# Root of the attention norm on the output projection's rows, in banks of its own; its weight in w_out

## The chip, the cores and the metric

The kernel runs on one core of a Trainium2 chip. Five engines work side by side, each with its own queue in fixed order: PE (matrix products and transposes, which write to PSUM), DVE and ACT (elementwise work, from SBUF and PSUM), POOL (elementwise work from SBUF, and DMA issues) and SP (DMA issues). They wait for one another by semaphores. The metric is the device time of one execution in microseconds; the time of a kernel is the median of three runs.

## The reference, cut to what matters

One decoder layer over 1024 tokens of width 1024, in float32. The token mixer has two halves of width 512, windowed attention with sinks and a gated recurrence (HGRN2). Each is normalised, then both go through one output projection:

```python
attn = sliding_window_sink_attention(aq, ak, av, attn_sinks[l])
attn = rmsnorm(attn, attn_out_w[l])          # y * rsqrt(mean(y*y) + eps) * w, over 512 columns
...
rec = rmsnorm(rec, hg_norm_w[l]) * jax.nn.silu(hg.reshape(B, T, HG_HEADS, HG_HEAD_DIM))
mix = jnp.concatenate([attn, rec], axis=-1) @ w_out[l]
x = x + g1 * rmsnorm(mix, post_w_mix[l])
h = rmsnorm(x, pre_w_mlp[l]) * (1.0 + sc2) + sh2
u = jnp.square(jax.nn.relu(h @ w_up[l]))
x = x + g2 * rmsnorm(u @ w_down[l], post_w_mlp[l])
```

The root of the attention norm is one number for each token; its weight is one number for each of the 512 columns, which are rows 0 to 511 of `w_out`.

## The kernel before, in words

Every float32 operand of a large product is kept as a high and a low part, and a product is three PE products: high by high, high by low, low by high (`proj3`). A helper records every operation, so that all rows of the profile have one line (L39); they are told apart by tiles.

The 1024 tokens are eight row blocks (tb) of 128. The stages on PE follow one another and overlap at their seams: input projection and attention (to about 200 us), the recurrence's units (to about 390), the output projection (about 365 to 465), then the up and the down projection of the channel mixer, which are arranged in seven products of blocks, to 1085.

**Attention** is a generator with four pieces for each row block; value projections (`pv`) are put between the pieces of different blocks to fill PE. The output of a block, `oT`, is transposed: columns on the partitions, tokens along the free dimension. Its norm takes these steps: ACT squares `oT` (`sqa`); DVE multiplies `oT` by the norm weight into `a3` (profile: `q<-oT,c_attw`); DVE sums the squares over four column blocks (`sqr`); PE transposes that (`ssp`); DVE sums to one number for each token (`ssc`); POOL makes the root (`t_att`, `r_att`); DVE puts it on a diagonal (`dg`); PE multiplies a matrix of ones by this diagonal, which spreads the root over all partitions (`rb`); DVE multiplies `a3` by it (`q<-q,rb`).

**Output projection.** `load_wo` splits `w_out` into parts, DVE and POOL making the low parts in turn. `op_prep` splits the attention (part 0) and the recurrence (part 1) of a row block; `op_mm` puts both parts of one half of the 1024 output columns into one bank (`po`): part 0 starts the sum, part 1 goes on with it. `out_proj` then has ACT square the bank, POOL make the root, DVE multiply the bank by root and weight (into `mixn`), add `x`, and so on to the normalised row block for the channel mixer.

**Transposes for the channel mixer.** `second_raw(0)` transposes row blocks 0 to 3, `second_raw(1)` blocks 4 to 7: eight tiles (`x2T`) of four transposes each, which ACT reads (`bt..h`) and then DVE or ACT reads (`h`).

**PSUM** has eight banks of 128 × 512 float32. The pool of `mm_ps` has two, that of `tp_ps` five, that of `a_ps` one. Scores, `pT`, `oT`, `po` and most `x2T` tiles take theirs from `tp_ps` in turn; `ssp`, `rb` and every third `x2T` tile (2 and 5) take the one of `a_ps`. A tile waits until the last reader of the bank's former tile is done.

**The order on each engine** is written out by hand up to the start of attention. From there on (`pin(False, ...)`) a scheduler sets it when the program is built, by its own idea of the times; what is moved in the source can therefore move other instructions as well. On the chip each engine takes its instructions in that order.

Of the kernel before, what the change touches and what calls it, by code (L numbers as in the profile page):

```python
# [47 lines left out]
def hybrid_layer(ctx: ExitStack, tc: tile.TileContext, I, out, dbg=None):  # L48
    nc = tc.nc
    ACT, DVE, POOL, PE, SP = (Queue(tc, e) for e in (nc.scalar, nc.vector, nc.gpsimd, nc.tensor, nc.sync))  # L50
# [9 lines left out]
    tiny1 = ctx.enter_context(tc.tile_pool(name="tiny1", bufs=1, side="right"))  # L60
# [25 lines left out]
    def t_(name, shape=(P, 512), dt=F32):  # L86
        return T2.tile(list(shape), dt, tag="t2", name=name)
# [4 lines left out]
    def tp_ps(name):  # L92
        return pb.tile([P, 512], F32, tag="b", name=name)
# [21 lines left out]
    ident, cT, bT, prew1, prew2 = (tab[:, a:b] for a, b in ((0, P), (P, 136), (136, 184), (184, 192), (192, 200)))  # L115
    ones = const.tile([P, P], F32, tag="ones", name="ones")
# [5 lines left out]
    mhalf = tiny0.tile([P, 8], F32, tag="mhalf", name="mhalf")  # L122
# [119 lines left out]
    def load_raw(mk, name, src, eng=None):  # L242
        rw = mk(name)
        (eng or SP).dma_start(rw, src)
        return rw

    def load_split(mk, name, src, eng=None, raw=None):
        hi, lo = mk(name + "h", dt=F32R), mk(name + "l", dt=F32R)
        for c in range(0, src.shape[1], 512):
            rw = load_raw(raw_, f"{name}r{c}", src[:, c:c + 512]) if raw is None else raw  # L250
            hc = hi[:, c:c + 512]
            ACT.activation(hc, rw, AF.Copy)
            (eng or DVE).tensor_tensor(lo[:, c:c + 512], rw, hc.bitcast(F32), ALU.subtract)
        return hi, lo

    gw1 = const.tile([P, D], F32, tag="gw1", name="gw1")
# [260 lines left out]
    attw = cload("attw", [P, 4], pool=tiny1)  # L517
    mle = cload("mle", [P, P], I32, pool=XA)
    fle = cload("fle", [P, P], pool=XA)
    attT = [None] * TB  # L520
    kTs, vs = {}, {}

    def attention(tb):
# [11 lines left out]
        aw = q  # L535
        a3 = aw.rearrange("p (m t) -> p m t", m=4)
# [5 lines left out]
        for mp in range(2):  # L542
            scs = [tp_ps(f"sc{tb}_{mp}_{g}").rearrange("p (m j) -> p m j", m=2) for g in range(2)]
            for m in range(2):
                for src in (tb - 1, tb) if tb else (tb,):
                    for g in range(2):
# [3 lines left out]
                                  start=True, stop=True)  # L550
# [48 lines left out]
        DVE.tensor_tensor(a3, o_ps.rearrange("p (m t) -> p m t", m=4), attw.unsqueeze(2).broadcast_to([P, 4, P]), ALU.mult)  # L599
        sqr = small.tile([P, P], F32, tag="sqr", bufs=1, name=f"sqr{tb}")  # L600
        DVE.tensor_reduce(sqr, sq.rearrange("p (m t) -> p t m", m=4), AX.X, ALU.add)
        ssp = pa.tile([P, 512], F32, tag="aps", name=f"ssp{tb}")
        PE.transpose(ssp[:, 0:P], sqr, ident)
        ssc = small.tile([P, 1], F32, tag="ssc", name=f"ssc{tb}")
        DVE.tensor_reduce(ssc, ssp[:, 0:P], AX.X, ALU.add)
        r = rstd_of(ssc, 512, 1, f"att{tb}")
        dg = small.tile([P, P], F32, tag="dg", bufs=1, name=f"dg{tb}")
        DVE.tensor_scalar(dg, ident, r[:, 0:1], None, ALU.mult)
        yield
        rb = pa.tile([P, 512], F32, tag="aps", name=f"rb{tb}")  # L610
        PE.matmul(rb[:, :P], lhsT=ones, rhs=dg, start=True, stop=True)
        DVE.tensor_tensor(a3, a3, rb[:, :P].unsqueeze(1).broadcast_to([P, 4, P]), ALU.mult)
        attT[tb] = aw
        yield

    def step(tb):
# [3 lines left out]
    att = [attention(tb) for tb in range(TB)]  # L620
# [15 lines left out]
    for tb in range(4):  # L636
        eng = DVE if tb < 2 else POOL
# [71 lines left out]
    aps = pa.tile([P, 512], F32, tag="aps", name="aps")  # L709
# [155 lines left out]
    wo = [[], []]  # L865
    op_mx, op_ps = {}, {}

    wo_raw = {}

    def wo_block(half, k):  # L870
        return I["w_o"][k][:, half * 512:half * 512 + 512]

    def load_wo(half, ks=range(KB)):
        for k in ks:
            wo[half].append(load_split(hT_, f"wo{k}_{half}", wo_block(half, k), eng=POOL if k % 2 else DVE,
                                       raw=wo_raw.pop((half, k), None)))

    def op_prep(tb, part):
        if (tb, part) in op_mx:
# [18 lines left out]
    def op_mm(tb, half, part, mk=None):  # L898
        if (tb, half, part) in op_ps:
            return  # L900
        op_ps[tb, half, part] = True
        if part == 0:
            op_ps[tb, half] = (mk or tp_ps)(f"po{tb}_{half}")
        proj3(op_ps[tb, half], op_mx[tb, part], wo[half][4 * part:4 * part + 4], part == 0, part == 1)

    units = [(h, th) for h in range(4) for th in range(2)]
    for kind in "fqg":
# [33 lines left out]
    r7 = next(proj)  # L941
    cores.append(head_core(*units[7], r7))
    load_wo(0)

    pin(True, SP)
# [55 lines left out]
    X2 = x2ctx.enter_context(tc.tile_pool(name="poolX2", bufs=1))  # L1001
# [2 lines left out]
    xn2 = [None] * TB  # L1004

    def out_proj(tb):
        for part in range(2):
            op_prep(tb, part)
            for half in range(2):
                op_mm(tb, half, part)  # L1010
        pst = [op_ps[tb, half] for half in range(2)]
        t = X2.tile([P, D], F32, tag="mixn", bufs=4, name=f"mixn{tb}")
        sso = small.tile([P, 2], F32, tag="ssx", name=f"sso{tb}")
        for half in range(2):
            ACT.activation(t[:, half * 512:half * 512 + 512], pst[half], AF.Square, accum_out=sso[:, half:half + 1])
        ss = small.tile([P, 1], F32, tag="ss1", name=f"sso1{tb}")
        POOL.tensor_tensor(ss, sso[:, 0:1], sso[:, 1:2], ALU.add)
        r = rstd_of(ss, D, 1, f"o{tb}")
        ssp = small.tile([P, 2], F32, tag="ssx2", name=f"ssp2{tb}")
        xs = []  # L1020
        for half in range(2):
            hs = slice(half * 512, half * 512 + 512)
            xr = t_(f"xr{tb}_{half}")
            SP.dma_start(xr, I["x"][tb * P:(tb + 1) * P, hs])
            DVE.scalar_tensor_tensor(t[:, hs], pst[half], r[:, 0:1], gw1[:, hs], ALU.mult, ALU.mult)
            DVE.tensor_tensor(xr, xr, t[:, hs], ALU.add)
            nc.gpsimd.dma_start(x1d[:, hold[tb, half]] if (tb, half) in hold else out[tb * P:(tb + 1) * P, hs], xr)
            ACT.activation(t[:, hs], xr, AF.Square, accum_out=ssp[:, half:half + 1])
            xs.append(xr)
        ss2 = small.tile([P, 1], F32, tag="ss1", name=f"ssp{tb}")  # L1030
        POOL.tensor_tensor(ss2, ssp[:, 0:1], ssp[:, 1:2], ALU.add)
        r2 = rstd_of(ss2, D, 1, f"p{tb}")
        for half in range(2):
            ACT.activation(t[:, half * 512:half * 512 + 512], xs[half], AF.Copy, scale=r2[:, 0:1])
        xn2[tb] = t
# [54 lines left out]
    for tb in range(5):  # L1090
        out_proj(tb)
# [497 lines left out]
    for step, (_, t, k) in enumerate(order):  # L1589
        n = ORDER[k]  # L1590
        key, first, th, half = PLAN[n]
# [11 lines left out]
        if k >= 3 and t < 3:  # L1603
            tb = t + 4 * th
# [139 lines left out]
```

## Time and profile before

| | |
|---|---|
| median of three runs | 1099.94 us (1099.77 to 1101.99) |
| span of the profiled execution | 1097.6 us |
| instructions of the profiled execution | 16208 |
| mean granted PE clock | 0.996 of full speed |
| PE, DVE, ACT, POOL busy | 98%, 72%, 53%, 34% of the span |
| DMA | 203.37 MB, mean 185 GB/s |

The span runs from the first to the last instruction of the execution; the run's own time holds about 2.3 us beside it, taken against the median. Busy shares are means over stages: the table of stretches in the prediction shows them apart. In rows of the timeline the first number is the start, the second the duration, and the bracket names the engine's idle time before it and what ended that. The ends of PE's products are modelled, so that the start of the next instruction says more than a row's duration.

### The profile page before, as it was taken

The page shows a single profiled execution, that of the slowest core. Times are in us where ns is not written, and L with a number is a line of the kernel's source. Part 1 is how long each engine was busy: PE and PEld are TensorE (multiplying, and loading weights), DVE is VectorE, ACT ScalarE, POOL GpSimd, SP SyncE. Part 2 cuts the span into 40 slices and gives each one's busy share as a digit, 9 for nine tenths or more (in the row PEclk, how much of TensorE's full clock was granted, in tenths as well). Part 3 has the DMA queues.
Part 4 walks back from the last instruction along what each step waited for, and adds up shares of the span by engine and source line. Part 5 has one row for each costly group of instructions (what it writes and reads, how often), then busy time and mean ns, then how long its engine had stood idle before and what let it go on. Part 6 is the DMA issues. An engine that isn't in the chain of part 4 may idle for free.

```text
span 1097.6 us, 16208 instructions
## 1 busy us (share of the span) xinstructions
PE 1076.2 (98%) x5547; PEld 878.2 (80%) x5547; DVE 795.1 (72%) x1323; ACT 584.6 (53%) x1206; POOL 373.2 (34%) x499
## 2 busy tenths in 40 slices
PE   8999999999999999999999999999999999999995
PEld 6788776778888888888888888888888888888884
DVE  4365777878865574559776767876767787899876
ACT  3445544364565764566655555556664543555434
POOL 1153211033324663432543444533333333310014
PEclk9999999999999999999999999999999999999998
DMA  9701301534310352324577676767998888998537
GB/s 347 265 7 57 117 1 43 181 101 140 125 56 11 108 182 96 125 79 144 194 246 249 233 259 227 257 216 244 320 364 289 275 299 259 337 308 272 169 76 131
DMA packets 101587, 203.37 MB, mean 185 GB/s; under 512 B 13025, under 2 KB 13681, under 8 KB 101505
## 3 DMA queue, kind: packets, MB, share of 16 engines
q1 hardware_dynamic: 85968, 154.52, 41.4%
q0 software_dynamic: 15392, 47.57, 14.3%
q8 instruction: 43, 0.70, 0.3%
q14 instruction: 40, 0.32, 0.1%
q10 hardware_dynamic: 144, 0.26, 0.1%
HBM read 147.25 MB, written 55.05 MB: 184 GB/s over the span
## 4 chain that ended last, share of the span: by engine, by line
PE 92%; DVE 3%; ACT 1%; DMA 1%; POOL 1%; issue 1%; SPq 0%; DVEq 0%; POOLq 0%; ACTq 0%
PE pda L39 16%; PE pua L39 14%; PE pdc L39 8%; PE po L39 8%; PE puc L39 7%; PE pu L39 4%; PE pdb L39 4%; PE pq L39 4%; PE phg L39 4%; PE phq L39 3%; PE pub L39 3%; PE phf L39 3%; PE pv L39 3%; PE pk L39 2%; PE o L39 1%; PE sc L39 1%
## 5 line engine op out<-in xcount | busy, mean ns | idle before, releaser
L39 POOL TENSOR_TENSOR b<-b,b 128x512 f32<-128x512 f32 x64 | 89.6, 1400 | 222.8 <-DMA b<-w_dn 222.4
L39 ACT ACTIVATE dw<-dwr 128x512 fp32r<-128x512 f32 x72 | 45.4, 630 | 46.5 <-DMA dwr<-td 32.4
L39 ACT ACTIVATE s<-s 128x512 f32<-128x512 f32 x84 | 53.0, 631 | 31.8 <-DVE s L39 30.5
L39 DVE TENSOR_TENSOR dw<-dwr,dw 128x512 fp32r<-128x512 f32 x72 | 53.6, 744 | 9.0 <-ACT dw L39 8.9
L39 DVE TENSOR_TENSOR acc<-pda,acc 128x512 f32<-128x512 f32 x68 | 46.5, 684 | 13.7 <-PE pda L39 13.3
L39 POOL DMA_DIRECT2D td<-b x64 | 36.3, 567 | 21.6 <-POOL b L39 18.7
L39 POOL TENSOR_TENSOR rrf<-ssf,mhalf 128x1 f32<-128x1 f32 x7 | 7.9, 1253 | 95.3 <-DVE ssf L39 95.3
L39 DVE TENSOR_TENSOR wt<-s,wt 128x512 fp32r<-128x512 f32 x42 | 37.2, 886 | 2.6 <-ACT wt L39 2.5
L39 ACT ACTIVATE s<-pua 128x512 f32<-128x512 f32 x28 | 16.7, 598 | 39.4 <-PE pua L39 33.9
L39 ACT ACT_TABLE_LOAD x28 | 35.9, 1283 | 1.2 <-PEq L1737 0.7
L39 DVE SCALAR_TENSOR_TENSOR macc<-wada,cs,macc 128x512 f32<-128x512 f32 x42 | 33.7, 803 | 3.4 <-DMA wada<-wada 2.9
L39 POOL DMA_DIRECT2D b<-w_dn x64 | 34.4, 540 | 0.0
L39 POOL TENSOR_TENSOR comb<-comb,rd 128x512 f32<-128x512 f32 x8 | 11.7, 1458 | 63.3 <-DVE rd L39 44.2
L39 PE MATMUL pua<-bt_0h,wt 128*128 128x512 f32 x84 | 32.7, 389 | 0.0
L39 PE MATMUL pua<-bt_1h,wt 128*128 128x512 f32 x84 | 32.7, 389 | 0.0
L39 PE MATMUL pua<-bt_3h,wt 128*128 128x512 f32 x84 | 32.7, 389 | 0.0
L39 PE MATMUL pua<-bt_2h,wt 128*128 128x512 f32 x84 | 32.7, 389 | 0.0
L39 DVE TENSOR_TENSOR wt<-a,wt 128x512 fp32r<-128x512 f32 x42 | 31.0, 738 | 0.9 <-ACT wt L39 0.9
L39 DVE TENSOR_TENSOR acc<-pdc,acc 128x512 f32<-128x512 f32 x36 | 24.6, 684 | 8.5 <-PE pdc L39 8.4
L39 ACT ACTIVATE wt<-s 128x512 fp32r<-128x512 f32 x42 | 26.3, 626 | 8.2 <-DVE s L39 8.0
L39 PE MATMUL pda<-dw,du_6h 128*128 128x512 f32 x96 | 29.6, 389 | 0.0
L39 PE MATMUL pda<-dw,du_7h 128*128 128x512 f32 x96 | 29.5, 389 | 0.0
(757 smaller groups left out, 3746.1 us busy)
## 6 DMA issues: line engine op xcount, KB each, us to landing
dur<-ud SPq DMA_DIRECT2D x112, 256.0 KB, 4.5
wada<-wada SPq DMA_DIRECT2D x64, 256.0 KB, 3.5
b<-w_dn POOLq DMA_DIRECT2D x64, 256.0 KB, 5.2
td<-b POOLq DMA_DIRECT2D x64, 256.0 KB, 3.3
dwr<-td SPq DMA_DIRECT2D x64, 256.0 KB, 4.3
a<-w_u SPq DMA_DIRECT2D x56, 256.0 KB, 4.4
dwr<-w_dn SPq DMA_DIRECT2D x48, 256.0 KB, 4.5
ud<-s SPq DMA_DIRECT2D x42, 256.0 KB, 3.6
```

What stands on the lines that cost most here:

```text
L39: ins = op(*args, **kw)
```

## The change

The root is no longer put on the attention output. `a3` becomes a plain copy of `oT` by ACT; `rb`, `dg` and both DVE multiplications go; the root of each token is kept in `ratt`, one column for each row block. Since the sum over columns of one token's attention is linear, the root can be put on the rows of the projected attention half, and the norm weight on the rows of `w_out`. So `load_wo` scales rows 0 to 511 of `w_out` while splitting them, all four low parts on DVE. `op_mm` gives each part of each half a bank of its own, four for a row block; ACT copies the part 0 banks into `mixn` with the root as scale, DVE adds the part 1 banks, ACT squares the sum (writing into the part 1 bank, which is done with), and the multiplication by root and weight reads SBUF.

```diff
@@ attention
-        DVE.tensor_tensor(a3, o_ps..., attw.unsqueeze(2).broadcast_to([P, 4, P]), ALU.mult)
-        sqr = small.tile([P, P], F32, tag="sqr", bufs=1, name=f"sqr{tb}")
+        ACT.activation(a3, o_ps.rearrange("p (m t) -> p m t", m=4), AF.Copy)
+        attT[tb] = aw
+        sqr = small.tile([P, P], F32, tag="sqr", bufs=2, name=f"sqr{tb}")
         DVE.tensor_reduce(sqr, sq.rearrange("p (m t) -> p t m", m=4), AX.X, ALU.add)
+        yield
         ssp = pa.tile([P, 512], F32, tag="aps", name=f"ssp{tb}")
         PE.transpose(ssp[:, 0:P], sqr, ident)
         ssc = small.tile([P, 1], F32, tag="ssc", name=f"ssc{tb}")
         DVE.tensor_reduce(ssc, ssp[:, 0:P], AX.X, ALU.add)
-        r = rstd_of(ssc, 512, 1, f"att{tb}")
-        dg = small.tile([P, P], F32, tag="dg", bufs=1, name=f"dg{tb}")
-        DVE.tensor_scalar(dg, ident, r[:, 0:1], None, ALU.mult)
-        yield
-        rb = pa.tile([P, 512], F32, tag="aps", name=f"rb{tb}")
-        PE.matmul(rb[:, :P], lhsT=ones, rhs=dg, start=True, stop=True)
-        DVE.tensor_tensor(a3, a3, rb[:, :P].unsqueeze(1).broadcast_to([P, 4, P]), ALU.mult)
-        attT[tb] = aw
+        ms = small.tile([P, 1], F32, tag="rs1", name=f"t_att{tb}")
+        POOL.tensor_scalar(ms, ssc, 1.0 / 512, EPS, ALU.mult, ALU.add)
+        POOL.tensor_tensor(ratt[:, tb:tb + 1], ms, mhalf[:, :1], ALU.pow)
         yield
@@ load_wo
-            wo[half].append(load_split(hT_, f"wo{k}_{half}", wo_block(half, k), eng=POOL if k % 2 else DVE,
-                                       raw=wo_raw.pop((half, k), None)))
+            raw = wo_raw.pop((half, k), None)
+            if k > 3:
+                wo[half].append(load_split(hT_, f"wo{k}_{half}", wo_block(half, k), eng=POOL if k % 2 else DVE, raw=raw))
+                continue
+            hi, lo = hT_(f"wo{k}_{half}h", F32R), hT_(f"wo{k}_{half}l", F32R)
+            if raw is None:
+                raw = load_raw(raw_, f"wo{k}_{half}r", wo_block(half, k))
+            ACT.activation(hi, raw, AF.Copy, scale=attw[:, k:k + 1])
+            DVE.scalar_tensor_tensor(lo, raw, attw[:, k:k + 1], hi.bitcast(F32), ALU.mult, ALU.subtract)
+            wo[half].append((hi, lo))
@@ op_mm
-        op_ps[tb, half, part] = True
-        if part == 0:
-            op_ps[tb, half] = (mk or tp_ps)(f"po{tb}_{half}")
-        proj3(op_ps[tb, half], op_mx[tb, part], wo[half][4 * part:4 * part + 4], part == 0, part == 1)
+        op_ps[tb, half, part] = (mk or tp_ps)(f"po{tb}_{half}_{part}")
+        proj3(op_ps[tb, half, part], op_mx[tb, part], wo[half][4 * part:4 * part + 4])
@@ out_proj
             for half in range(2):
                 op_mm(tb, half, part)
-        pst = [op_ps[tb, half] for half in range(2)]
+                if part == 0:
+                    ACT.activation(t[:, halves[half]], op_ps[tb, half, 0], AF.Copy, scale=ratt[:, tb:tb + 1])
         sso = small.tile([P, 2], F32, tag="ssx", name=f"sso{tb}")
         for half in range(2):
-            ACT.activation(t[:, half * 512:half * 512 + 512], pst[half], AF.Square, accum_out=sso[:, half:half + 1])
+            pst, th = op_ps[tb, half, 1], t[:, halves[half]]
+            DVE.tensor_tensor(th, pst, th, ALU.add)
+            ACT.activation(pst, th, AF.Square, accum_out=sso[:, half:half + 1])
...
-            DVE.scalar_tensor_tensor(t[:, hs], pst[half], r[:, 0:1], gw1[:, hs], ALU.mult, ALU.mult)
+            DVE.scalar_tensor_tensor(t[:, hs], t[:, hs], r[:, 0:1], gw1[:, hs], ALU.mult, ALU.mult)
```

What the scheduler makes of it, at three places. First DVE in attention, around the norm of row block 3 (`sqr3` to `ssc3`), before:

```order
L39 TENSOR_TENSOR comb4_1598<-comb4_1598,rd4_1648 128x512 [waits DVE_49]
L39 TENSOR_TENSOR q3_866<-oT3_1746,c_attw_830 128x512 [waits Activation_49]
L39 TENSOR_REDUCE sqr3_1754<-sqa3_1751 128x128
L39 COPY kT5_1775<-pkT5_1773 128x128 [waits PE_49]
L39 TENSOR_REDUCE ssc3_1758<-ssp3_1756 128x1 [waits PE_49]
L39 TENSOR_SCALAR dg3_1764<-c_tab_97,r_att3_1762 128x128 [waits Pool_49]
```

and now:

```order
L39 COPY kT5_1748<-pkT5_1746 128x128 [waits PE_49]
L39 RECIPROCAL rd4_1627<-den4_1625 128x8 [waits DVE_49]
L39 TENSOR_REDUCE sqr3_1737<-sqa3_1734 128x128 [waits Activation_49]
L39 TENSOR_TENSOR comb4_1577<-comb4_1577,rd4_1627 128x512 [waits DVE_49]
L39 TENSOR_REDUCE ssc3_1833<-ssp3_1831 128x1 [waits PE_49,Pool_49]
```

The product with the weight and the diagonal are gone, and `kT` and `rd` stand ahead of `sqr` where `comb` and `q` stood. On PE, `ssp3` now stands ahead of the score products of block 5 (`sc5`), behind six value products:

```order
L39 MATMUL pv2_1929<-whv4l_1656,hhi4_0_606 128x512
L39 MATMUL pv2_1929<-whv4h_1655,hlo4_0_607 128x512
L39 MATMUL pv2_1929<-whv5h_1661,hhi5_0_645 128x512
L39 MATMUL pv2_1929<-whv5l_1662,hhi5_0_645 128x512
L39 MATMUL ssp3_1831<-c_tab_97,sqr3_1737 128x128 [waits DVE_49]
L39 MATMUL pv2_1929<-whv5h_1661,hlo5_0_646 128x512
L39 MATMUL sc5_0_0_1751<-kT4_1575,qT5_1744 128x128 [waits Activation_49]
```

Before, half of a score group stood ahead of it, and `rb3` stood between the scores and `pT4_0`. Last ACT at the first transposes of the channel mixer (`x2T0_0` to `x2T0_7`, read into `bt1_..` and `bt2_..`), with the projection of row block 4 (`po4`, `mixn4`), before:

```order
L39 ACTIVATE bt1_0h_4724<-x2T0_0_4718,sh2_996,a2_995 128x512 [waits PE_49]
L39 ACTIVATE bt1_1h_4735<-x2T0_1_4729,sh2_996,a2_995 128x512 [waits PE_49]
L39 ACTIVATE bt1_2h_4746<-x2T0_2_4740,sh2_996,a2_995 128x512 [waits PE_49]
L39 ACTIVATE bt1_3h_4757<-x2T0_3_4751,sh2_996,a2_995 128x512 [waits PE_49]
L39 ACTIVATE bt2_0h_4768<-x2T0_4_4762,sh2_996,a2_995 128x512 [waits PE_49]
L39 ACTIVATE mixn4_4638,sso4_4639<-po4_0_4578 128x512 [waits PE_49]
L39 ACTIVATE mixn4_4638,sso4_4639<-po4_1_4591 128x512
L39 ACTIVATE bt2_1h_4779<-x2T0_5_4773,sh2_996,a2_995 128x512
```

and now:

```order
L39 ACTIVATE bt1_0h_4707<-x2T0_0_4701,sh2_997,a2_996 128x512 [waits PE_49]
L39 ACTIVATE bt1_1h_4718<-x2T0_1_4712,sh2_997,a2_996 128x512 [waits PE_49]
L39 ACTIVATE bt1_2h_4729<-x2T0_2_4723,sh2_997,a2_996 128x512
L39 ACTIVATE bt1_3h_4740<-x2T0_3_4734,sh2_997,a2_996 128x512 [waits PE_49]
L39 ACTIVATE bt2_0h_4751<-x2T0_4_4745,sh2_997,a2_996 128x512 [waits PE_49]
L39 ACTIVATE bt2_1h_4762<-x2T0_5_4756,sh2_997,a2_996 128x512
L39 ACTIVATE bt2_2h_4773<-x2T0_6_4767,sh2_997,a2_996 128x512 [waits PE_49]
L39 ACTIVATE mixn4_4551<-po4_0_0_4556,ratt_836 128x512 [waits PE_49]
L39 ACTIVATE mixn4_4551<-po4_1_0_4570,ratt_836 128x512
```

Block 4's first reading of its banks moved from behind the fifth tile to behind the seventh, and its banks are now four: `po4_0_0`, `po4_1_0`, `po4_0_1` and `po4_1_1`. In the program as built, `x2T0_0`, `1`, `3`, `4`, `6` and `7` now have one and the same bank, where before `0` and `4` had one, `1` and `6` another and `3` and `7` a third; `2` and `5` have that of `a_ps` in both.

More of the change, by code (lines that the diff above doesn't have):

```diff
@@ L519, in hybrid_layer @@
     fle = cload("fle", [P, P], pool=XA)
+    ratt = tiny1.tile([P, TB], F32, tag="ratt", name="ratt")
     attT = [None] * TB
@@ L598, in attention @@
         ACT.activation(sq, o_ps, AF.Square)
-        DVE.tensor_tensor(a3, o_ps.rearrange("p (m t) -> p m t", m=4), attw.unsqueeze(2).broadcast_to([P, 4, P]), ALU.mult)
-        sqr = small.tile([P, P], F32, tag="sqr", bufs=1, name=f"sqr{tb}")
+        ACT.activation(a3, o_ps.rearrange("p (m t) -> p m t", m=4), AF.Copy)
+        attT[tb] = aw
+        sqr = small.tile([P, P], F32, tag="sqr", bufs=2, name=f"sqr{tb}")
         DVE.tensor_reduce(sqr, sq.rearrange("p (m t) -> p t m", m=4), AX.X, ALU.add)
+        yield
         ssp = pa.tile([P, 512], F32, tag="aps", name=f"ssp{tb}")
@@ L1006, in out_proj @@
     def out_proj(tb):
+        t = X2.tile([P, D], F32, tag="mixn", bufs=4, name=f"mixn{tb}")
+        halves = [slice(half * 512, half * 512 + 512) for half in range(2)]
         for part in range(2):
@@ L1010, in out_proj @@
                 op_mm(tb, half, part)
-        pst = [op_ps[tb, half] for half in range(2)]
-        t = X2.tile([P, D], F32, tag="mixn", bufs=4, name=f"mixn{tb}")
+                if part == 0:
+                    ACT.activation(t[:, halves[half]], op_ps[tb, half, 0], AF.Copy, scale=ratt[:, tb:tb + 1])
         sso = small.tile([P, 2], F32, tag="ssx", name=f"sso{tb}")
         for half in range(2):
-            ACT.activation(t[:, half * 512:half * 512 + 512], pst[half], AF.Square, accum_out=sso[:, half:half + 1])
+            pst, th = op_ps[tb, half, 1], t[:, halves[half]]
+            DVE.tensor_tensor(th, pst, th, ALU.add)
+            ACT.activation(pst, th, AF.Square, accum_out=sso[:, half:half + 1])
         ss = small.tile([P, 1], F32, tag="ss1", name=f"sso1{tb}")
```

## The prediction

> **What bounds the kernel now.** First the page: the busy shares, and the chain of work that ended last.
>
> ```profile
> PE 1076.2 (98%) x5547; PEld 878.2 (80%) x5547; DVE 795.1 (72%) x1323; ACT 584.6 (53%) x1206; POOL 373.2 (34%) x499
> PE 92%; DVE 3%; ACT 1%; DMA 1%; POOL 1%; issue 1%; SPq 0%; DVEq 0%; POOLq 0%; ACTq 0%
> ```
>
> PE sets the end. Only where PE stands idle, or has an instruction less or more to do, can the time move. So next comes PE's busy time by stage (columns after the stretch: its length, then busy time and instructions of PE, PEld, DVE, ACT and POOL, the granted clock, the DMA share and rate).
>
> ```profile
> 100.00:130.00 30.00, 28.48 (x191) 20.82 (x190) 22.91 (x52) 18.96 (x73) 7.91 (x14) 1.00 0.44 141
> 130.00:165.00 35.00, 34.99 (x236) 25.39 (x235) 26.85 (x63) 16.48 (x61) 6.58 (x9) 1.00 0.00 1
> 165.00:200.00 35.00, 34.05 (x179) 23.32 (x178) 27.88 (x53) 14.23 (x48) 5.35 (x8) 1.00 0.22 65
> 200.00:230.00 30.00, 28.27 (x124) 22.81 (x124) 23.94 (x40) 15.33 (x23) 6.68 (x8) 1.00 0.45 148
> 230.00:365.00 135.00, 135.00 (x878) 111.86 (x877) 98.84 (x178) 76.15 (x153) 51.27 (x57) 1.00 0.31 96
> 365.00:430.00 65.00, 64.98 (x344) 54.35 (x343) 36.50 (x78) 37.30 (x113) 35.11 (x53) 1.00 0.37 135
> 430.00:442.00 12.00, 11.73 (x66) 9.45 (x65) 8.74 (x12) 5.97 (x13) 3.49 (x5) 1.00 0.07 23
> 442.00:465.00 23.00, 23.00 (x103) 19.03 (x102) 12.18 (x17) 13.46 (x31) 11.45 (x23) 1.00 0.43 149
> 490.00:1000.00 510.00, 510.00 (x2252) 422.27 (x2251) 402.17 (x558) 281.01 (x480) 191.56 (x223) 1.00 0.77 261
> ```
>
> Attention (100 to 230) has 1.52 + 0.01 + 0.95 + 1.73 = 4.2 us of idle PE. From 230 on PE is dense, so whatever PE gains or loses up to 490 arrives at the end one for one; nothing later absorbs it. Who is waited for in attention, as the waits of PE name it (us in total, times, longest):
>
> ```profile
> PE rb L39 <- DVE dg L39: 1.6, 4, 0.6
> PE phg L39 <- ACT f L39: 1.3, 1, 1.3
> PE ssp L39 <- DVE sqr L39: 0.6, 2, 0.3
> PE pT L39 <- DVE comb L39: 0.4, 1, 0.4
> ```
>
> The change takes out rb, the product that spreads the root over the partitions.
>
> **Part 1, attention.** One row block of the steady stretch in the timeline (start, length, engine):
>
> ```profile
> 130.54 0.60 ACT L39 ACTIVATE sqa<-oT 128x512 f32<-128x512 f32 x1 [0.44 <-PE oT L39]
> ...
> 130.85 0.48 PE L39 MATMUL pv<-whv3l,hhi 128*128 128x512 f32 x1
> ...
> 131.18 0.69 DVE L39 TENSOR_TENSOR q<-oT,c_attw 128x512 f32<-128x512 f32 x1
> ...
> 131.78 1.04 DVE L39 TENSOR_REDUCE sqr<-sqa 128x128 f32<-128x512 f32 x1
> ...
> 132.88 0.33 PE L39 MATMUL ssp<-c_tab,sqr 128*128 128x128 f32 x1
> ...
> 134.48 0.29 DVE L39 TENSOR_SCALAR dg<-c_tab,r_att 128x128 f32<-128x128 f32 x1 [0.95 <-POOL r_att L39]
> ...
> 134.91 0.49 PE L39 MATMUL rb<-dg,ones 128*128 128x128 f32 x2
> ...
> 135.24 1.04 PE L39 MATMUL pT<-c_tab,comb 128*128 128x128 f32 x8
> ```
>
> rb starts at 134.91 and the next PE instruction at 135.24: it holds PE 0.33 us, and 8 of them 2.6 us. With it go its waits, 1.6 us. That makes 4.2 us.
>
> Its wait can come back at ssp, which still needs sqr. In the new order PE comes there after six value products (the first at 130.85, about 0.23 us each: 132.25), DVE after a kT copy instead of the q product. sqa ends at 131.14; the sqr of 1.04 us after it ends between 132.2 and 132.6. So ssp would wait 0 to 0.35 us. But it waits now too, unnamed: it starts 0.06 us after sqr's end at 132.82, some 0.28 us after PE was free. I take no difference. The named waits of ssp, pT and phg, 2.3 us in all, may shrink with the 1.65 us of DVE work (q, dg, q again) that each block loses, or the ssp wait may grow by 0.35 us a block, 2.8 us over eight. Ends of the gain: 1.4 and 6.5 us; taken 4.2, near the middle. ACT's extra copy of 0.60 us (as sqa, the same shape) stands ahead of qT, and the products of scores that need qT now come after seven value products, 0.23 us each, which cover it; uncovered it costs up to 0.6 us a block, which lies inside the low end. The root's write stays on POOL, and nothing on PE waits for it before the output projection.
>
> **Part 2, the weights of the projection.** For rows 0 to 3 of w_out the copy takes a scale, and all low parts go to DVE.
>
> ```profile
> L39 DVE TENSOR_TENSOR wo_0l<-wo_0r,wo_0h 128x512 fp32r<-128x512 f32 x4 | 4.1, 1050 | 1.6 <-ACT wo_0h L39 1.6
> ...
> L39 POOL TENSOR_TENSOR wo_0l<-wo_0r,wo_0h 128x512 fp32r<-128x512 f32 x4 | 5.6, 1388 | 0.5 <-ACT wo_0h L39 0.5
> ...
> L39 ACT ACTIVATE mixn<-po 128x512 f32<-128x512 f32 x8 | 4.6, 581 | 0.0
> ```
>
> Four of them come from POOL: 4 × 1.05 = 4.2 us more for DVE, which has 36 us free between 230 and 365, and 4 × 1.39 = 5.6 less for POOL. On PE: nothing. If the cover were gone, one late low part would stall the projection for about its 1.05 us.
>
> **Part 3, banks of the projection.** ACT copies each first product with the root as scale: 0.58 plain from PSUM, in the row just quoted, and 0.67 with a scale from SBUF, half of this one, the last step of row block 3:
>
> ```profile
> 427.13 1.34 ACT L39 ACTIVATE mixn<-xr,r_p 128x512 f32<-128x512 f32 x2 [1.25 <-POOL r_p L39]
> ```
>
> I take 0.65; 16 × 0.65 = 10 us. DVE adds the second (about 0.69, as q above): 16 × 0.69 = 11 us. Both engines are busy little more than half of 365 to 430, where PE is dense, so the work itself is hidden. Block 3, the last of the first group, is done one add later; it ends at 428.47 now, 2.2 us before PE asks for it (430.71, below). What is not hidden is the banks. Each row block now holds four of the pool's five rather than two.
>
> At the first group's transposes (x2T0, eight tiles of four) block 4 has all four: the new ACT order has its two scaled copies behind the seventh of the eight evacuations, and its DVE adds come later still. So six of the eight tiles (0, 1, 3, 4, 6, 7) go one after the other through the one bank that is left; 2 and 5 have the bank of attention. Before, three banks stood in turn. What one turn of a bank costs stands in the chain of waits:
>
> ```profile
> 424.97 5.90 PE po L39 x26
> 430.87 0.45 PE x2T L39 x4
> ...
> 431.35 0.79 ACT bt_0h L39
> ...
> 432.16 0.82 DVE h L39
> ...
> 433.00 0.69 DVE bt_0l L39
> ...
> 435.17 1.15 DVE bt_2l L39
> ```
>
> Transpose, ACT's copy, DVE's h, and the bank is free: 433.00 − 430.87 = 2.13 us. ACT and DVE read in turn, 0.02 us apart. Before, PE filled the time:
>
> ```profile
> 430.71 1.91 PE L39 MATMUL x2T<-c_tab,mixn 128*128 128x128 f32 x16
> 432.37 0.48 PE L39 MATMUL po<-wo_0h,mx 128*128 128x512 f32 x1
> ...
> 437.10 0.66 PE L39 MATMUL x2T<-c_tab,mixn 128*128 128x128 f32 x4 [0.21 <-DVE h L39]
> 437.82 0.50 PE L39 MATMUL po<-wo_1h,mx 128*128 128x512 f32 x1
> ```
>
> From 430.71 to 437.82 it did the 32 transposes and the 12 products of po5_0's second part, 12 × 0.227 (5.90 / 26) = 2.72 us. The transposes thus took 7.11 − 2.72 = 4.39 us. In the new order those 12 need a bank and stand behind x2T0_7. So: five turns of 2.13 = 10.65, the last tile 0.42 (1.66 / 4), and twice about 0.3 us where DVE's turn for bank 7's tile and a low part stands before the waited one: 11.7 us. The loss is 11.7 − 4.39 = 7.3 us. Low end: no queueing on DVE, 6.7. High end: low parts at the 1.15 us of bt_2l rather than 0.69, on three turns, 1.4 more: 8.7. After it all banks come free in time (block 4's copies end at about 442, before PE reaches them). The second group's transposes find six banks whose readers ended long before; nothing there.
>
> The Trainium skill, "Perfetto Trace Analysis", section Matmuls, wants independent matmul groups to rotate through different PSUM banks, so that evacuating one overlaps the next; section Optimization Strategy reads a gap that repeats as too little SBUF or PSUM. The row of 2.13 us a turn agrees. Taken as a case for this change, the first rule makes each half product's own bank free of cost, which is the last rival below.
>
> **Sum.** −4.2 + 7.3 = +3.1 us. The profiled execution spans 1097.6 us; the median of the runs is 2.3 us more. 1097.6 + 3.1 + 2.3 = **1103.0 us**, 0.28% slower. Own range 1101 to 1105.5.
>
> **Rivals.**
> *The wait moves to ssp* (0.17). The gain is 1.4 us, the time 1097.6 − 1.4 + 7.3 + 2.3 = 1105.8. For it: sqr ends after PE is free already now. Against: the q product that stood ahead of sqr is gone.
> *The gain covers the loss* (0.19), the case that isn't slower. DVE, at 27.88 of 35 us the second busiest in 165:200, is what attention's waits lead back to; with 13 us less to do there it lets PE go without a stop. Gain: 4.2 idle + 2.6 = 6.8, against a loss at its low end of 6.7: 1099.8, from 1098.4 to 1101. It decides from the point where the waits of ssp, pT and phg go as well. Against: the chain behind phg's 1.3 us ends in a DMA.
> *The clock falls* (0.04) in the thinned transposes.
>
> ```profile
> 1080.00:1085.00 5.00, 4.68 (x27) 3.93 (x25) 4.14 (x8) 4.38 (x9) 3.84 (x7) 1.00 0.81 115
> 1085.00:1090.00 5.00, 0.00 (x0) 0.00 (x0) 4.37 (x10) 1.87 (x7) 2.77 (x4) 0.86 1.09 168
> ```
>
> After PE's end at 1084.7 the clock stayed full for about 3.9 us: 0.86 over 5 us is 3.6 us at 1 and 1.4 at 0.5. In the transposes no gap is over 2.13 − 0.42 = 1.7 us. If it fell, one product of 12 at half speed costs 2.7 more: 1105.7. The Trainium skill, "TensorE: Matmul & The Clock Gate", section What's actually happening, halves the clock after an idle window of about 3.4 us; the trace agrees.
> *The banks cost nothing* (0.10): the chain on one bank does not form, because PE finds block 4's banks free when it gets there. Then 1097.6 − 4.2 + 2.3 = 1095.7. Against: the order on ACT is fixed when the program is built.
>
> **How the numbers follow.** Forecast 0.50. What can be told from no change is 0.2%, 2.2 us: under 1097.7 is faster, over 1102.1 slower. Faster: the last rival and a little of the second, 0.13. Slower: most of the forecast (0.38), 0.17 and 0.04, 0.59. Same: the rest, 0.28. The range that leaves out about a fifth: 1097.6 to 1106.8.
>
> **What would show it.** No rb and no wait for dg; PE's idle between 100 and 230 below 4.2 us and about 4 us earlier at 230. Then x2T0 tiles 1, 3, 4, 6 and 7 each waiting 1.2 to 1.7 us for DVE's h, some 11.7 us from the first transpose to the next po product, and ACT's copies of block 4 behind them. It is wrong if x2T takes under 9 us, if ssp waits in most blocks, or if PE idles anew after 230 at the projection for a low part, a copy or an add.

## The result, and the profile after

| | before | changed |
|---|---|---|
| median | 1100.14 us | 1123.42 us |
| lowest to highest of five runs | 1099.77 to 1101.99 | 1122.04 to 1126.47 |
| span of the profiled execution | 1097.6 us | 1124.7 us |

The change makes the kernel slower by 23.3 us: ratio 1.0212, 95% interval 1.0201 to 1.0223. The forecast was 1103.0 us with a range up to 1106.8. The direction was right; the size, 3 us forecast, was wrong by more than a factor of seven. The profiled execution of the changed kernel is the slowest of its five (1126.47 us): 2.1 us of its distance to the kernel before are there already 20 us after the start, where PE waits longer for `x` and the clock is at half for 3.4 us.

First the page of the changed kernel, busy shares and the chain of work that ended last:

```profile
PE 1096.2 (97%) x5531; PEld 879.4 (78%) x5531; DVE 788.2 (70%) x1319; ACT 601.8 (54%) x1230; POOL 359.9 (32%) x495
PE 88%; POOL 3%; ACT 3%; DVE 2%; issue 2%; DMA 1%; SPq 0%; DVEq 0%; POOLq 0%; ACTq 0%
```

PE has 16 records fewer than before and is busy 20 us longer. Waiting would not show as busy time. The same busy times by stage (columns as before: length, PE, PEld, DVE, ACT, POOL, granted clock, DMA):

```profile
100.00:130.00 30.00, 29.27 (x199) 21.39 (x198) 22.69 (x50) 20.96 (x75) 9.17 (x18) 1.00 0.45 141
130.00:165.00 35.00, 34.85 (x238) 25.26 (x238) 23.44 (x54) 19.16 (x72) 5.34 (x9) 1.00 0.00 1
165.00:200.00 35.00, 34.95 (x185) 25.51 (x182) 28.45 (x52) 15.70 (x45) 5.73 (x9) 1.00 0.28 91
200.00:230.00 30.00, 30.00 (x159) 23.75 (x158) 20.24 (x34) 16.09 (x25) 6.37 (x7) 1.00 0.47 151
...
430.00:442.00 12.00, 5.93 (x28) 4.25 (x27) 6.40 (x8) 5.68 (x8) 2.55 (x3) 0.63 0.17 58
442.00:465.00 23.00, 21.15 (x82) 16.44 (x81) 12.27 (x19) 14.39 (x31) 8.59 (x18) 0.82 0.27 91
...
600.00:1000.00 400.00, 400.00 (x1730) 324.31 (x1729) 296.45 (x412) 213.25 (x362) 147.06 (x179) 1.00 0.81 270
```

The last stretch of the kernel before:

```profile
600.00:1000.00 400.00, 400.00 (x1767) 331.29 (x1766) 315.10 (x435) 216.14 (x367) 144.23 (x175) 1.00 0.82 278
```

Three things stand here. Idle PE in attention fell from 4.2 to 0.9 us, as forecast. Between 430 and 442 PE is half idle, and the granted clock falls to 0.63 there and 0.82 in the stretch behind it. And 600 to 1000 has 400 us of dense PE at full clock with no wait, as before, yet fewer products: 1730, where there were 1767, so that one takes 2.1% longer on the average.

The waits of PE from 0.4 us on, except those of the start, are the five forecast ones of x2T for DVE's h, the old one of pT, and three that the forecast did not have: u (of the recurrence) for k4n, the first transposes for the last step of block 3 (`mixn`), and the output projection for ACT.

```profile
PE x2T L39 <- DVE h L39: 7.4, 5, 1.7
...
PE u L39 <- ACT k4n L39: 1.0, 1, 1.0
PE pT L39 <- DVE comb L39: 0.4, 1, 0.4
PE x2T L39 <- ACT mixn L39: 0.4, 1, 0.4
PE po L39 <- ACT po L39: 0.4, 1, 0.4
```

The chain through the first transposes shows one turn of the bank after the other:

```profile
432.95 1.10 PE x2T L39 x4
...
434.08 0.79 ACT bt_1h L39
...
434.89 0.82 DVE h L39
...
435.75 1.13 PE x2T L39 x4
```

A turn takes 2.8 us (435.75 − 432.95) rather than the 2.13 of the forecast: the four transposes take 1.1 us, not 0.45, at half clock.

Last, what the down projection's products cost, the same 48 of the chain in the kernel before

```profile
822.59 10.88 PE pda L39 x48
```

and in the changed one

```profile
843.12 11.20 PE pda L39 x48
```

10.88 / 48 = 0.2267 us a product, 11.20 / 48 = 0.2333. Nothing was changed there. By landmarks of the two traces, the changed kernel is 3.65 us ahead at the first product of the output projection, 7.5 us behind at the last transpose of the first group, 13.8 behind at the last of the second, 19.6 at the first product of the down projection and 26.5 at PE's end. The last 12.7 us, over some 600 us, come without a single wait: they are slower products.

### The profile page after: what moved, and what is told of

Its sections match the earlier page's. It is cut to its first block, busy times and chain, and to the rows that moved or that the text cites. A ratio compares the mean times of both kernels' runs of the same rounds, so it can differ in the third digit from the quotient of the medians.

```text
span 1124.7 us, 16211 instructions
## 1 busy us (share of the span) xinstructions
PE 1096.2 (97%) x5531; PEld 879.4 (78%) x5531; DVE 788.2 (70%) x1319; ACT 601.8 (54%) x1230; POOL 359.9 (32%) x495
## 3 DMA queue, kind: packets, MB, share of 16 engines
q0 software_dynamic: 15392, 47.57, 14.2%
## 4 chain that ended last, share of the span: by engine, by line
PE 88%; POOL 3%; ACT 3%; DVE 2%; issue 2%; DMA 1%; SPq 0%; DVEq 0%; POOLq 0%; ACTq 0%
PE pda L39 16%; PE pua L39 14%; PE pdc L39 8%; PE puc L39 7%; PE pu L39 4%; PE pdb L39 4%; PE pq L39 4%; PE phg L39 3%; PE pub L39 3%; PE phq L39 3%; PE phf L39 3%; PE pv L39 3%; PE po L39 3%; PE pk L39 2%; PE oT L39 1%
## 5 line engine op out<-in xcount | busy, mean ns | idle before, releaser
L39 DVE TENSOR_TENSOR dw<-dwr,dw 128x512 fp32r<-128x512 f32 x72 | 53.3, 741 | 11.7 <-ACT dw L39 11.7
L39 DVE TENSOR_TENSOR wt<-a,wt 128x512 fp32r<-128x512 f32 x42 | 33.7, 802 | 1.5 <-ACT wt L39 1.5
L39 DVE TENSOR_TENSOR s<-puc,s 128x512 f32<-128x512 f32 x14 | 9.7, 691 | 30.6 <-issue 28.0
L39 ACT ACTIVATE comb<-comb,nm 128x128 f32<-128x128 f32 x64 | 24.8, 388 | 11.1 <-DVE sd L39 11.1
```

What stands on the lines that cost most here:

```text
L39: ins = op(*args, **kw)
```

## The experiments

The theory after the result had four parts. **A**: the 32-byte tile of the roots (`ratt`) pushed all tiles of its side of SBUF by 32 bytes; the operand that streams through PE in a product and the weights that are loaded for the next one then lie at another distance, and that makes the product slower. **C**: the first transposes stand on one bank, as forecast. **D**: the clock falls there because PE works too little over several microseconds. Besides, attention gained more than forecast. Rival **B** was that the new order or the banks slow all products.

### Addresses

Two runs separate A from B: the change with another size of that tile, and the kernel before with nothing but a tile.

```diff
-    ratt = tiny1.tile([P, TB], F32, tag="ratt", name="ratt")
+    ratt = tiny1.tile([P, 2 * TB], F32, tag="ratt", name="ratt")
```

> The changed kernel with the tile of the roots made 16 columns wide (64 bytes) rather than 8 (32 bytes); nothing else differs, and every engine's order is the same. Theory A, addresses: the new 32-byte tile moved every tile on its side of SBUF by 32 bytes, and in 2603 of 4089 wide products the operand that streams and the weights loaded next then lie 32 bytes apart against a 64-byte step; those products follow each other after 0.2333 us, not 0.2267, some 19 us in all. It expects all wide products at 0.2267 and a time of 1104 us (1102 to 1107). Theory B, the order or the banks slow all products: it expects no change, 1122 to 1126.

Measured: 1117.88 us, ratio 1.0165 (1.0149 to 1.0182). Every engine's order is that of the changed kernel, and 5.5 us went, so B alone can't hold; but products stayed slow, and the 19 us did not come back.

```diff
     attw = cload("attw", [P, 4], pool=tiny1)
+    tiny1.tile([P, 8], F32, tag="gap", name="gap")
```

> The kernel before with an unused tile of 32 bytes in the same place as the roots' tile; every engine's order stays that of the kernel before. Theory A expects products in 2605 pairs at 0.2333 us, and 1100.1 + 17 to 20 = 1117 to 1120 us, with no wait on PE that was not there before. Theory B expects 1100.

Measured: 1116.84 us, ratio 1.0154 (1.0137 to 1.0171), just under the expectation. A tile of 32 bytes that nothing reads or writes costs the kernel before 17 us. B has fallen for this part of the time. The chain of this run has the slow products of the changed kernel:

```profile
834.16 11.20 PE pda L39 x48
```

```diff
     tiny0 = ctx.enter_context(tc.tile_pool(name="tiny0", bufs=1))
+    tiny0.tile([P, 8], F32, tag="gap0", name="gap0")
...
+    tiny1.tile([P, 8], F32, tag="gap", name="gap")
```

> The kernel before with an unused tile of 32 bytes on either side of SBUF: every tile is off the 64-byte step, and all 4089 pairs are off it together. If only the distance between streaming operand and next weights counts (theory A1), 1100 us and 0.2267 a product, as before. If each address by itself counts (theory A2), all pairs are slow: 1100 + 4089 x 0.0067 = 1127 us or more.

Measured: 1110.45 us, ratio 1.0101 (1.0086 to 1.0116): neither of the two. The expectation had overlooked that one side of SBUF is filled from the bottom and the other from the top. The two tiles move their sides by +32 and −32 bytes, so the sides are 64 bytes apart, as in the run with 64 bytes. Both show the same picture, so a distance of 64 bytes counts too.

The next runs put the roots where they move nothing (the pool that lies last on its side), and 128 and 256 bytes wide where they were:

```diff
-    ratt = tiny1.tile([P, TB], F32, tag="ratt", name="ratt")
+    ratt = small.tile([P, TB], F32, tag="ratt", bufs=1, name="ratt")
```

> The changed kernel with the 32-byte tile of the roots in the pool that lies last on its side, so that no operand of a wide product is moved; every engine's order is that of the changed kernel. With 64 bytes of shift the products were still slow (0.2301 us a product on the average, against 0.2271 before). If the distance between the streaming operand and the next weights counts to more than 64 bytes (theory A3), all 4089 come back to 0.2271: 1117.9 - 4089 x 0.003 = 1105.6 us (1103 to 1108), and what is left over the kernel before is the transposes and the clock, less the gain of attention. If the products stay slow, the address has nothing to do with it: 1116 to 1123.

Measured: 1106.84 us, ratio 1.0060 (1.0048 to 1.0073), with the order of the changed kernel on every engine. 16.6 us of the 23.3 were addresses. The same 48 products:

```profile
829.89 10.88 PE pda L39 x48
```

> The changed kernel with the tile of the roots 128 bytes wide: operands and next weights are 128 bytes apart in the same 2603 pairs. If distances count only to 128 bytes, this is as the run with the roots elsewhere, 1103 to 1108. If they count to 512 bytes, the step between the weights of one operand, it is slow like the 32 and 64 byte tiles: 1112 to 1123.

Measured: 1122.39 us, ratio 1.0203 (1.0189 to 1.0217). 128 bytes are as bad as 32.

> The tile of the roots 256 bytes wide: the same 2603 pairs are 256 bytes apart, half of the 512 bytes between the weights of one operand. If distances count to 256 bytes only, products at 0.227 us and the time of the run with the roots elsewhere, 1105 to 1109; if to 512, slow products in those pairs and 1112 to 1124.

Measured: 1107.25 us, ratio 1.0065 (1.0048 to 1.0081), the time of the run with the roots elsewhere. 256 bytes are harmless.

From all these traces, matched with the addresses in the programs: the mean time from the start of a wide product to the start of the next, for pairs that stand next to each other and start less than 0.3 us apart, grouped by the address of the first one's streaming operand less that of the second one's weights, to 512 bytes. Pairs that lie on one side of SBUF keep distance 0 in every run; they are left out here except in the first line.

| distance, bytes | run | pairs matched | mean, ns |
|---|---|---|---|
| 0 | before | 3886 | 227.1 |
| +32 / −32 | changed | 1632 / 911 | 233.4 / 233.4 |
| +64 / −64 | roots 64 bytes | 1631 / 911 | 229.7 / 233.3 |
| 128, two directions | roots 128 bytes | 1633 / 911 | 232.7 / 232.9 |
| 256, the same two sets | roots 256 bytes | 1630 / 911 | 227.2 / 226.7 |

The whole program has 2603 such pairs, and 2603 × 6.3 ns = 16.4 us, what the medians show (16.6). Why reading at these distances costs time isn't shown. That it is a distance and not either address is shown by the 175 pairs of the changed kernel in which both lie 32 bytes off (228.8 ns, against 228.4 for those in which neither does). Two things stay open. The pairs at distance 0 are a little slower too in the shifted runs: the same 1341 pairs take 227.3 ns in the kernel before and 228.4 with the unused tile, 1.5 us in all. And in nearly all pairs a product's own weights and the next one's lie on the same side of SBUF, so that the table can't tell which of the two counts; the few in which they don't, some 30 of each kind in a run, say the next one's in the changed kernel (235.0 ns when only these are 32 bytes off, 229.3 when only the own are) and the own in the run with 64 bytes (225.8 and 230.7).

### The clock

In the run with the roots elsewhere the records of the clock have 13.7 us at half speed from 430.3 on; in the kernel before there are none before PE's end. Spare products fill the gaps, with the roots elsewhere as well (parts of the edit):

```diff
                 PE.transpose(pst[:, j * P:(j + 1) * P], xn2[th * 4 + j][:, kb * P:(kb + 1) * P], ident)
+            if not th and kb < 7:
+                for i in range(6 if kb % 3 == 0 else 3):
+                    PE.matmul(fill_ps, lhsT=wo[0][0][0][:, 0:P], rhs=wo[0][1][0], start=True, stop=True)
...
+    fill_ps = mm_ps("fill")
+    pin(True, PE)
     second_raw(0)
+    pin(False, PE)
```

> The changed kernel with the roots elsewhere, and 30 spare products (28 of them inside the gaps, 0.21 to 0.23 us each) put between the eight tiles of the first transposes, into a bank that nobody reads, so that PE is busy there; PE's order is fixed over these tiles alone, and they stand in the order 0 to 7. It takes no wait away. Theory D, the clock falls because PE works too little over several us, though no single gap is over 1.7 us: the clock stays at 1, a turn of the bank takes 2.1 us rather than 2.8, the products after it come at 0.227 us, and the time is 5 to 8 us below that of the run with the roots elsewhere: 1099 to 1102. If the half clock cost nothing there, or fell for another reason, it stays at 1106 to 1109.

Measured: 1103.83 us, ratio 1.0033 (1.0020 to 1.0045), 3.0 us below the run with the roots elsewhere, though PE does 30 products more. The sign is theory D's; the size, half of what it said, lies outside its range. From 425 to 445, without the spare products and with them:

```profile
425.00:445.00 20.00, 11.70 (x47) 8.42 (x46) 10.77 (x14) 10.18 (x17) 6.36 (x9) 0.66 0.13 47
```

```profile
425.00:445.00 20.00, 17.47 (x87) 13.26 (x87) 12.35 (x17) 11.62 (x19) 6.03 (x7) 1.00 0.10 33
```

The clock stays at 1. The transposes take 13.5 rather than 15.0 us from the first to the last, and the time from there to the second group's, dense products, 41.7 rather than 43.0. The Trainium skill's "TensorE: Matmul & The Clock Gate" describes a related case in its section "A second HAM failure mode: psum-queue depth-cycling": in a kernel that cycled through PSUM banks, PE rested briefly and so often between groups of products that its clock went back and forth. This trace agrees in that short rests were enough; here the clock fell once and stayed down for 13.7 us. These are stretches of 3.4 us of the run with the roots elsewhere, up to the fall and behind it:

```profile
423.60:427.00 3.40, 2.61 (x15) 2.01 (x14) 0.25 (x1) 2.14 (x6) 2.05 (x5) 1.00 0.38 154
427.00:430.40 3.40, 1.07 (x8) 0.59 (x6) 1.62 (x3) 1.80 (x4) 0.00 (x0) 0.99 0.47 157
430.40:433.80 3.40, 1.97 (x8) 1.56 (x8) 3.24 (x4) 1.30 (x2) 1.27 (x1) 0.50 0.01 2
```

PE was busy for 1.07 of 3.40 us, in pieces with rests of 1.4 and 1.7 us, and then had half the clock.

How much work keeps the clock can be read from all the traces together. The stretches of half clock at the transposes last 3.41, 13.65 or 17.07 us, one, four or five times 3.413 us; so each trace can be cut into stretches of that length, in step with its clock records. Behind the first 30 us, these are the ones at full clock in which PE was least busy:

| run | stretch, us | PE busy of 3.41 us | clock behind it |
|---|---|---|---|
| five buffers (next section) | 430.60 to 434.01 | 0.66 | half |
| roots elsewhere | 426.92 to 430.33 | 1.15 | half |
| roots 256 bytes | 427.99 to 431.40 | 1.28 | half |
| roots 64 bytes | 425.55 to 428.96 | 1.39 | half |
| five buffers (next section) | 427.19 to 430.60 | 1.48 | full |
| roots 128 bytes | 428.45 to 431.86 | 1.59 | half |
| changed | 429.60 to 433.01 | 1.63 | half |
| roots 256 bytes | 424.58 to 427.99 | 1.67 | full |

Every other stretch at full clock, in any run and up to PE's end, has 1.9 us or more and no fall behind it. So in these runs the clock falls when PE was busy for less than about half of such a stretch, however the rests are cut up; one stretch, of 1.48 us, goes against it. Whether transposes count for the clock as other products do is not told apart here.

### The banks

`mixn` has four buffers, so block 4's copies out of its banks write where block 0's result lies until all eight tiles have been transposed. That is what holds the banks. A fifth buffer takes it away:

```diff
-        t = X2.tile([P, D], F32, tag="mixn", bufs=4, name=f"mixn{tb}")
+        t = X2.tile([P, D], F32, tag="mixn", bufs=5, name=f"mixn{tb}")
```

> The 64-byte tile, and five buffers for mixn rather than four: row block 4's copies out of its banks no longer wait for the first group's transposes to have read mixn0. If the transposes stood on one bank because of that (theory C), their waits for DVE (7.4 us in all) go, the granted clock stays at 1 between 430 and 465, and the time is 8 to 11 us below that of the 64-byte kernel: 1093 to 1096. If the banks are not freed by it, or the clock falls for another reason, it stays within 2 us of the 64-byte kernel.

Measured, with the 64-byte tile: 1111.35 us, ratio 1.0108 (1.0091 to 1.0125), 6.5 us below the 64-byte run; 8 to 11 were expected, and the 1093 to 1096 had also taken the products of that run to be fast. The five waits are gone, and another stands in their place:

```profile
426.16 2.51 PE L39 MATMUL x2T<-c_tab,mixn 128*128 128x128 f32 x21 [0.67 <-ACT mixn L39]
432.55 0.66 PE L39 MATMUL x2T<-c_tab,mixn 128*128 128x128 f32 x4 [3.88 <-DVE h L39]
434.11 0.79 PE L39 MATMUL po<-wo_1h,mx 128*128 128x512 f32 x1 [0.90 <-DVE h L39]
```

The transposes now go through at once, but with its buffer free the scheduler puts block 4's whole chain ahead of their evacuation on ACT and DVE, and DVE's first `h` starts at 431.69. One gap of 3.9 us follows, and the clock records show one stretch of 3.4 us at half. So a run with the second half of block 4's work held back (parts of the edit):

```diff
+        yield                                  # out_proj, after the squares
...
+    next(outs[4])                              # ahead of second_raw(0)
     second_raw(0)
-    for tb in range(5, TB):
-        out_proj(tb)
+    with tc.issue_after(marks["h2"]):          # the last h of second_raw(0)
+        finish(outs[4])
+    for tb in range(5, TB):
+        finish(outs[tb])
```

> As the run with the roots elsewhere, with five buffers for mixn, and the second half of row block 4's work (from the root on) put behind the evacuation of the first transposes on ACT and DVE. Theory C (one bank, because copies wait behind the transposes, and with five buffers alone because block 4's chain stands ahead of the evacuations): PE waits under 2 us in all between 425 and 445, the granted clock stays at 1, and first work of the up projection comes 7 to 9 us before that of the kernel before: 1091 to 1094 us. If the stall has another cause, it stays above 1098.

Measured, with five buffers and the roots elsewhere: 1097.45 us, ratio 0.9968 (0.9956 to 0.9981): 3.0 us faster than the kernel before and 9.4 below the run with the roots elsewhere, but not the 1091 to 1094 expected. The clock stays at 1. PE waits 2.4 us between 425 and 445, a little over what was expected:

```profile
427.56 2.51 PE L39 MATMUL x2T<-c_tab,mixn 128*128 128x128 f32 x21 [0.78 <-ACT mixn L39]
430.91 0.65 PE L39 MATMUL x2T<-c_tab,mixn 128*128 128x128 f32 x4 [0.84 <-DVE h L39]
432.36 0.50 PE L39 MATMUL po<-wo_1h,mx 128*128 128x512 f32 x1 [0.79 <-DVE h L39]
```

Theory C holds: from the first transpose to the second group's first it is 47.5 us here, 45.3 in the kernel before and 57.9 in the run with the roots elsewhere. In this execution PE also started 1.1 us later than before (a wait for `x` of 2.8 us at the start), which is no part of the change.

### Attention alone

The output projection of before under the changed attention and `w_out`, with the roots elsewhere (a part of the edit; the copies and adds of `out_proj` go too). This kernel leaves out the root of the attention norm:

```diff
-        op_ps[tb, half, part] = (mk or tp_ps)(f"po{tb}_{half}_{part}")
-        proj3(op_ps[tb, half, part], op_mx[tb, part], wo[half][4 * part:4 * part + 4])
+        op_ps[tb, half] = (mk or tp_ps)(f"po{tb}_{half}")      # part 0 only, as before
+        proj3(op_ps[tb, half], op_mx[tb, part], wo[half][4 * part:4 * part + 4], part == 0, part == 1)
```

> The attention and w_out parts of the change with the output projection of before (one bank for a half, no copies, no adds). It leaves out the root of the attention norm; nothing else of the computation. It prices parts 1 and 2 alone. On record they were worth 4.2 us (1.4 to 6.5): 1096 (1093.5 to 1098.5). The 64-byte run came to the first product of the output projection 8.1 us before the kernel before, with slow products on the way, which would make it 1091 to 1092.

Measured: 1094.12 us, ratio 0.9949 (0.9935 to 0.9963): parts 1 and 2 are worth 6.4 us, at the upper end of the range on record and short of the 8 to 9 us that the 64-byte run suggested. Its trace is 8.9 us ahead of the kernel before at the first product of the output projection and 7.1 at the first transpose. Between the two stands a wait that the kernel before does not have:

```profile
PE u L39 <- ACT k4n L39: 1.5, 1, 1.5
```

PE, now early, waits there (at 362 us) for a copy of the recurrence, and ACT, which makes it, has waited 2.8 us for POOL.

## Why the prediction was right or wrong, point by point

**What bounds the kernel: right as far as it went.** PE set the end, and what PE lost in the transposes came out at the end. What failed is the sentence "From 230 on PE is dense, so whatever PE gains or loses up to 490 arrives at the end one for one". It takes for granted that the dense products themselves keep their duration, 0.227 us. Nothing in the working asked what a product's duration depends on. The change adds `ratt`, 32 bytes, and 16.6 us of the 23.3 come from that tile's place alone. No term of the sum, no rival and no bound had it. "One for one" failed in a small way too: of what attention gained, 1.5 us went into the new wait for k4n at 362.

**Part 1: the mechanism was right, the size too small.** Forecast 4.2 us, measured 6.4. The waits of ssp didn't grow: it starts 0.46 us after the product ahead of it in attention alone, 0.50 in the steady blocks before, so "no difference" was right, and idle PE between 100 and 230 fell to 1.2 us. The term that was mis-sized is that of one block. Before, the period from ssp to ssp in the steady stretch is 12.5 us:

```profile
145.42 0.33 PE L39 MATMUL ssp<-c_tab,sqr 128*128 128x128 f32 x1
145.90 1.61 PE L39 MATMUL sc<-kT,qT 64*128 64x128 f32 x24
147.44 0.49 PE L39 MATMUL rb<-dg,ones 128*128 128x128 f32 x2
...
157.95 0.33 PE L39 MATMUL ssp<-c_tab,sqr 128*128 128x128 f32 x1
```

and with the changed attention 11.9:

```profile
141.67 0.33 PE L39 MATMUL ssp<-c_tab,sqr 128*128 128x128 f32 x1
142.16 2.06 PE L39 MATMUL sc<-kT,qT 64*128 64x128 f32 x32
144.15 1.09 PE L39 MATMUL pT<-c_tab,comb 128*128 128x128 f32 x8
...
153.59 0.33 PE L39 MATMUL ssp<-c_tab,sqr 128*128 128x128 f32 x1
```

That is 0.61 us a block, of which rb is 0.33. The rest goes with the scores: they stand in one piece of 32, where before 8 stood ahead of ssp and 24 behind it, and each time that scores begin behind a value product, 0.33 to 0.41 us pass between the two starts rather than 0.23. The order of PE showed that the pieces were joined; the working gave it no price. As an estimate, if every block gains as much: 8 × 0.61 = 4.9, and 3.0 of idle PE between 100 and 230, less the 1.5 for k4n, make 6.4.

**Part 2: right.** PE waits for no low part of `w_out` in any run. In attention alone, a low part on POOL (1.28 us) and a high part on ACT stand shortly ahead of the copy k4n that PE waits for; whether they lengthen that wait isn't shown.

**Part 3: the one bank was right, and its price was too low.** "Tiles 1, 3, 4, 6 and 7 each waiting 1.2 to 1.7 us for DVE's h" is nearly what the waits show: 7.4 us, five times, four of them from 1.36 to 1.72 us and that of tile 4, which has tile 5 ahead of it, 0.86. "Some 11.7 us from the first transpose to the next po product" was 15.6 (429.91 to 445.51). With the clock held up by spare products it is 14.2 (424.53 to 438.77). Of the 2.5 us over the forecast, 0.8 are the wait for block 3, which the working had as covered by 2.2 us, and 0.45 a wait for block 4's copy ("banks come free in time"); a turn of the bank, 2.4 to 2.6 us with the spare products between, is the rest. Forecast 7.3 us; the distance from attention alone to the spare-product run, in which the spare products may hold up some transposes, is 1103.83 − 1094.12 = 9.7.

**The clock: the rival was given 0.04, and it came true.** The step that failed is "In the transposes no gap is over 2.13 − 0.42 = 1.7 us". The gaps had that length (at most 1.72 us) and the clock fell all the same, for 13.7 to 17.1 us. The working read the clock's rule from the one long rest at the program's end, as a longest gap. The runs show a busy share in its place: falls behind stretches of 3.41 us with 0.7 to 1.6 us of PE's work. Its price, 2.7 us, was near the 3.0 of the spare products.

**The rivals.** The wait did not move to ssp. The gain does not cover the loss. The banks did cost. That leaves the sum, by medians: −6.4 (attention and w_out) + 9.7 (the banks, clock held) + 3.0 (the clock) + 16.6 (addresses) = 22.9, of 23.3 measured. Each term is one run less another, so that the sum has to close but for 0.4, by which the medians of the kernel before differ; what bears the account are the terms, and of these 9.7 holds all else that the new output projection and the spare products cost.

## What to carry to other kernels

A new tile, however small, can move every tile behind it on its side of SBUF. Compare the addresses of the operands of the dense products before and after a change, streaming operands against weights; here a tile of 32 bytes cost 17 us, and the roots in a pool that lies last left the products as they were. Where a change makes a ring of buffers longer-lived, look for what else that ring holds back: four banks a block were no trouble, the fourth buffer of `mixn` made them one. Several short rests of PE in a row can cost more than their sum, since the clock may fall with them: add up PE's busy time over a few microseconds, and don't only look for the longest gap.

## What the runs showed of the hardware that was not expected

A wide product (128 × 128 weights, 512 columns, four bytes an element) starts 0.2267 us after the one ahead of it when the streaming operand and the weights are at the same place to 256 bytes, and 0.2297 to 0.2334 us when they are 32, 64 or 128 bytes apart; at 64 bytes the two directions, which are also two sets of products, differ (0.2297 one way, 0.2333 the other). At full clock, with PE dense, this shows nowhere as a wait: only in the spacing of the products, and in PE's busy time, which grew by 20 us for 16 records fewer (the half clock has a part in that).

The granted clock fell to a half for 17.1 us in the changed kernel, with no rest of PE over 1.72 us at the transposes, and a single rest of 3.9 us brought 3.4 us at half. In six of the runs it fell behind a stretch of 3.41 us in which PE was busy for 0.66 to 1.63 us; of the stretches that it outlasted all but one had 1.67 us or more.
